# Sixteen unrolled turns rewritten as a hardware loop with staggered semaphore resets, in a log-softmax backward kernel

## The chip, the cores and the metric

The kernel runs on one core of one Trainium2 chip. The metric is the device time of one execution in microseconds (us), the median of several. Before the change it is 1867 us. Profiles are of one execution.

## The reference

The inputs are `y` (a log-softmax) and `dy`, both 8 x 1024 x 8192 float32. The output has the same shape.

```python
def reference(y, dy):
    softmax_x = np.exp(y)
    sum_dy = np.sum(dy, axis=-1, keepdims=True)
    return (dy - softmax_x * sum_dy).astype(np.float32)
```

Each input is 268 MB and has to be read once; the output is as large and has to be written once. That makes 805 MB, and one exponential, one multiply and two adds per element, one of them for the sum.

## The kernel before

The 8192 rows are cut into 32 groups of 256 rows: 128 partitions with two rows (R = 2) each, so one tile of a group is 128 x 16384 float32, 8.39 MB. There are two tiles for `dy` (`x_ts`), for even groups ("A") and odd groups ("B"), which also hold the result, and one buffer for `y`. A group's sum of `dy` is taken by VectorE for the first row of a partition and by ScalarE for the second. Then, piece by piece, ScalarE takes the exponential of `y` in place and VectorE writes exp(y) * (-sum) + dy over `dy`. Two groups share the `y` buffer, so the two halves of B's `y` are loaded as soon as the pieces of A's `y` that lie there have been used. All transfers are issued from SyncE.

```python
    def load_dy(g, x):
        nc.sync.dma_start(out=x[:], in_=dy_v[g])

    def load_y(g, at, lo, hi):
        nc.sync.dma_start(out=y_t[:, at + lo : at + hi], in_=y_v[g][:, lo:hi])

    def compute(x, s_t, at, r, pieces):
        for b, e in pieces:
            xs = slice(r * D + b, r * D + e)
            ys = slice(at + r * D + b, at + r * D + e)
            nc.scalar.activation(y_t[:, ys], y_t[:, ys], EXP)
            nc.vector.scalar_tensor_tensor(
                out=x[:, xs], in0=y_t[:, ys], scalar=s_t[:, r : r + 1],
                in1=x[:, xs], op0=ALU.mult, op1=ALU.add)

    for g in range(0, G, 2):                  # 16 turns, unrolled
        load_dy(g, x_ts[0])
        load_y(g, SHIFT, 0, W)
        s_t = sums(x_ts[0])
        for r in range(R):
            compute(x_ts[0], s_t, SHIFT, r, PIECES_A)
        load_dy(g + 1, x_ts[1])
        s_t = sums(x_ts[1])
        for r in range(R):
            load_y(g + 1, 0, r * D, (r + 1) * D)
            compute(x_ts[1], s_t, 0, r, PIECES_B)
        for j in range(2):
            nc.sync.dma_start(out=out_v[g + j], in_=x_ts[j][:])
    # ... (cut: views, pools, sums())
```

Of the kernel before, what the change touches and what calls it, by code (L numbers as in the profile page):

```python
# [1 line left out]

# [5 lines left out]


EXP = mybir.ActivationFunctionType.Exp  # L10
COPY = mybir.ActivationFunctionType.Copy
ALU = mybir.AluOpType


@with_exitstack
def kernel(
    ctx: ExitStack,
    tc: tile.TileContext,
    y: bass.AP,
    dy: bass.AP,  # L20
    out: bass.AP,
):





    nc = tc.nc
    P = nc.NUM_PARTITIONS
    fp32 = mybir.dt.float32  # L30

    N, D = y.flatten_outer_dims().shape
    R = 2
    W = R * D
    G = N // (P * R)
    assert N == G * P * R and D == 8192 and G % 2 == 0
    SHIFT = 3840

    PIECES_A = [(0, 1024), (1024, D - SHIFT), (D - SHIFT, D)]
    PIECES_B = [(0, 2048), (2048, 5120), (5120, D)]  # L40

    y_v = y.flatten_outer_dims().rearrange("(g p r) d -> g p (r d)", p=P, r=R)
    dy_v = dy.flatten_outer_dims().rearrange("(g p r) d -> g p (r d)", p=P, r=R)
    out_v = out.flatten_outer_dims().rearrange("(g p r) d -> g p (r d)", p=P, r=R)

    pool = ctx.enter_context(tc.tile_pool(name="pool", bufs=1))
    stats = ctx.enter_context(tc.tile_pool(name="stats", bufs=3))
    x_ts = [pool.tile([P, W], fp32, name=f"x{j}") for j in range(2)]
    y_t = pool.tile([P, SHIFT + W], fp32, name="y_t")

    def load_dy(g, x):
        nc.sync.dma_start(out=x[:], in_=dy_v[g])  # L52

    def sums(x):
        s_t = stats.tile([P, R], fp32, name="s_t")
        second_t = stats.tile([P, 1], fp32, name="second_t")
        nc.vector.tensor_reduce(  # L57
            out=s_t[:, 0:1], in_=x[:, :D], axis=mybir.AxisListType.X, op=ALU.add, negate=True
        )
        nc.scalar.activation(x[:, D:], x[:, D:], COPY, accum_out=second_t[:])  # L60
        nc.vector.tensor_scalar(  # L61
            out=s_t[:, 1:2], in0=second_t[:], scalar1=-1.0, scalar2=None, op0=ALU.mult
        )
        return s_t
# [10 lines that stand above are left out]
                out=x[:, xs],  # L75
                in0=y_t[:, ys],
                scalar=s_t[:, r : r + 1],
                in1=x[:, xs],
                op0=ALU.mult,
                op1=ALU.add,  # L80
            )

    for g in range(0, G, 2):
        load_dy(g, x_ts[0])
        load_y(g, SHIFT, 0, W)
        s_t = sums(x_ts[0])
        for r in range(R):
            compute(x_ts[0], s_t, SHIFT, r, PIECES_A)
        load_dy(g + 1, x_ts[1])
        s_t = sums(x_ts[1])  # L90
        for r in range(R):
            load_y(g + 1, 0, r * D, (r + 1) * D)
            compute(x_ts[1], s_t, 0, r, PIECES_B)
        for j in range(2):
            nc.sync.dma_start(out=out_v[g + j], in_=x_ts[j][:])


# [1 line left out]
_INS = ['y', 'dy']  # L99
_OUTS = [((8, 1024, 8192), 'float32')]  # L100


# [23 lines left out]
```

## Time and profile before

| | before |
|---|---|
| time, median of 3 | 1867.12 us (1866.89 to 1867.31) |
| bytes over the transfer queue | 805.31 MB |
| queue's share of the span | 99.8% |
| VectorE busy, ScalarE busy | 46%, 37% |
| one turn of two groups | 116.4 us |

The kernel is bound by its transfers. In lines of the profile, DVE is VectorE, ACT is ScalarE, SPq is SyncE's instruction stream, which issues all transfers, L73 is line 73 of the kernel, and x6 means that six instructions stand in one line. A transfer has landed when its last part has arrived.

### The profile page before, as it was taken

The page shows a single profiled execution, that of the slowest core. Times are in us where ns is not written, and L with a number is a line of the kernel's source. Part 1 is how long each engine was busy: PE and PEld are TensorE (multiplying, and loading weights), DVE is VectorE, ACT ScalarE, POOL GpSimd, SP SyncE. Part 2 cuts the span into 40 slices and gives each one's busy share as a digit, 9 for nine tenths or more (in the row PEclk, how much of TensorE's full clock was granted, in tenths as well). Part 3 has the DMA queues.
Part 4 walks back from the last instruction along what each step waited for, and adds up shares of the span by engine and source line. Part 5 has one row for each costly group of instructions (what it writes and reads, how often), then busy time and mean ns, then how long its engine had stood idle before and what let it go on. Part 6 is the DMA issues. An engine that isn't in the chain of part 4 may idle for free.

```text
span 1866.1 us, 843 instructions
## 1 busy us (share of the span) xinstructions
DVE 857.9 (46%) x256; ACT 689.3 (37%) x257; POOL 0.2 (0%) x4
## 2 busy tenths in 40 slices
DVE  2907429074290742807328073280732806338163
ACT  2606326063260532605326053260523605235152
POOL 0000000000000000000000000000000000000000
DMA  9999999999999999999999999999999999999998
GB/s 427 427 427 427 431 444 429 427 434 443 427 434 438 425 435 442 428 429 431 440 431 430 438 427 436 437 440 427 430 438 435 428 437 428 438 435 434 434 428 386
DMA packets 16134, 805.36 MB, mean 432 GB/s; under 512 B 1792, under 2 KB 1792, under 8 KB 1792
## 3 DMA queue, kind: packets, MB, share of 16 engines
q1 hardware_dynamic: 16128, 805.31, 99.8%
q14 instruction: 6, 0.05, 0.0%
HBM read 536.87 MB, written 268.44 MB: 432 GB/s over the span
## 4 chain that ended last, share of the span: by engine, by line
DMA 65%; DVE 14%; another core or an unknown queue 10%; ACT 9%; issue 0%; DVEq 0%; ACTq 0%; SPq 0%
DMA x<-in_dy_dram 31%; DMA out_dram<-x 30%; DVE x L74 14%; ACT x L60 6%; ACT y_t L73 3%; DMA y_t<-in_y_dram 3%; DVEq L121 0%; ACTq L121 0%; SPq L52 0%; ACTq L73 0%; ACTq L60 0%
## 5 line engine op out<-in xcount | busy, mean ns | idle before, releaser
L74 DVE SCALAR_TENSOR_TENSOR x<-y_t,s_t,x 128x1024 f32<-128x1024 f32 (+2 forms) x192 | 579.4, 3059 | 257.5 <-ACT y_t L73 257.5
L57 DVE TENSOR_REDUCE s_t<-x 128x1 f32<-128x8192 f32 x32 | 277.8, 8682 | 721.9 <-DMA x<-in_dy_dram 721.9
L73 ACT ACTIVATE y_t<-y_t 128x1024 f32<-128x1024 f32 (+2 forms) x192 | 460.1, 2466 | 280.0 <-DMA y_t<-in_y_dram 280.0
L60 ACT ACTIVATE x<-x 128x8192 f32<-128x8192 f32 x32 | 225.0, 7030 | 863.2 <-DMA x<-in_dy_dram 863.2
L60 ACT ACTIVATION_READ_ACCUMULATOR x<-x 128x1 f32 x32 | 6.0, 187 | 0.0
L61 DVE TENSOR_SCALAR s_t<-second_t 128x1 f32<-128x1 f32 x32 | 4.6, 143 | 0.0
L60 ACT ACT_TABLE_LOAD x1 | 1.3, 1283 | 0.7 <-PEq L110 0.7
L110 POOL MEMSET const-uint8-127<- 128x1 uint8 x1 | 0.1, 102 | 0.0
L110 POOL MEMSET const-bfloat16-1.0<- 128x1 bf16 x1 | 0.1, 101 | 0.0
L110 POOL MEMSET const-float32-0.0<- 128x1 f32 x1 | 0.1, 98 | 0.2 <-issue 0.2
L110 POOL MEMSET const-float32-1.0<- 128x1 f32 x1 | 0.1, 98 | 0.0
## 6 DMA issues: line engine op xcount, KB each, us to landing
y_t<-in_y_dram SPq DMA_DIRECT2D x32, 4096.0 KB, 22.1
x<-in_dy_dram SPq DMA_DIRECT2D x32, 48.4
out_dram<-x SPq DMA_DIRECT2D x32, 32.6
y_t<-in_y_dram SPq DMA_DIRECT2D x16, 57.5
```

The source lines that it names most:

```text
L57: nc.vector.tensor_reduce(out=s_t[:, 0:1], in_=x[:, :D], axis=mybir.AxisListType.X, op=ALU.add, negate=True)
L60: nc.scalar.activation(x[:, D:], x[:, D:], COPY, accum_out=second_t[:])
L61: nc.vector.tensor_scalar(out=s_t[:, 1:2], in0=second_t[:], scalar1=-1.0, scalar2=None, op0=ALU.mult)
L73: nc.scalar.activation(y_t[:, ys], y_t[:, ys], EXP)
L74: nc.vector.scalar_tensor_tensor(out=x[:, xs], in0=y_t[:, ys], scalar=s_t[:, r : r + 1], in1=x[:, xs], op0=ALU.mult, op1=ALU.add,)
L110: nc = _bacc.Bacc("TRN2", target_bir_lowering=False, num_devices=1)
```

## The change

The intent is a short program: one body in a hardware loop in place of sixteen copies. The loop that is built resets its semaphores, the counters by which engines wait for each other, between turns. Instead of a full barrier at the loop's end, the staggered form cuts the body into four stages with `stage_boundary()`. In the built program an engine enters a stage only when all engines have signalled the end of the stage two back, and a stage's semaphores are reset meanwhile.

```diff
-    for g in range(0, G, 2):
+    with tc.For_i(0, G, 2, iteration_sync="staggered") as g:
         load_dy(g, x_ts[0])
         load_y(g, SHIFT, 0, W)
+        tc.stage_boundary()
         s_t = sums(x_ts[0])
         for r in range(R):
             compute(x_ts[0], s_t, SHIFT, r, PIECES_A)
         load_dy(g + 1, x_ts[1])
+        tc.stage_boundary()
         s_t = sums(x_ts[1])
         for r in range(R):
             load_y(g + 1, 0, r * D, (r + 1) * D)
             compute(x_ts[1], s_t, 0, r, PIECES_B)
+        tc.stage_boundary()
         for j in range(2):
             nc.sync.dma_start(out=out_v[g + j], in_=x_ts[j][:])
```

What it builds to around the stores, told from the built program (waits and signals; "stage 1" is compute A and the load of B's dy, counted from 0):

```
SyncE    wait B's dy landed; signal "I have finished stage 1"
SyncE    wait until all five engines have signalled stage 1
SyncE    store A
SyncE    wait store A landed
SyncE    store B (waits for VectorE's last step of compute B)

VectorE  ... last step of compute B (stage 2)
VectorE  signal "I have finished stage 1"
ScalarE  ... last exponential of compute B (stage 2)
ScalarE  signal "I have finished stage 1"
```

## The prediction

> **What bounds the kernel now.** I read the page first. Its engine line, the DMA line of the forty slices, the queue line and the memory line are:
>
> ```profile
> DVE 857.9 (46%) x256; ACT 689.3 (37%) x257; POOL 0.2 (0%) x4
> DMA  9999999999999999999999999999999999999998
> q1 hardware_dynamic: 16128, 805.31, 99.8%
> HBM read 536.87 MB, written 268.44 MB: 432 GB/s over the span
> ```
>
> No engine is busy for half of the span, while the one transfer queue has work for 99.8% of it. The time is the bytes: 805.31 MB in 1866.1 us. What matters about any change here is whether the queue ever runs empty.
>
> Second, the timeline of one turn of two groups from the middle (start, duration, engine). A start behind "<-DMA" marks a landing.
>
> ```profile
> 857.53 14.32 ACT L73 ACTIVATE y_t<-y_t 128x1024 f32<-128x1024 f32 x6 [12.23 <-DMA y_t<-in_y_dram]
> ...
> 865.20 9.25 SPq L67 DMA_DIRECT2D y_t<-in_y_dram  x2
> 876.83 7.03 ACT L60 ACTIVATE x<-x 128x8192 f32<-128x8192 f32 x1 [4.98 <-DMA x<-in_dy_dram]
> ...
> 878.25 30.03 SPq L95 DMA_DIRECT2D out_dram<-x  x2
> ...
> 886.54 7.22 ACT L73 ACTIVATE y_t<-y_t 128x2048 f32<-128x2048 f32 x3 [2.59 <-DMA y_t<-in_y_dram]
> ...
> 896.56 7.22 ACT L73 ACTIVATE y_t<-y_t 128x2048 f32<-128x2048 f32 x3 [2.80 <-DMA y_t<-in_y_dram]
> ...
> 915.87 0.34 SPq L52 DMA_DIRECT2D x<-in_dy_dram  x1
> ...
> 935.16 0.33 SPq L52 DMA_DIRECT2D x<-in_dy_dram  x1
> ...
> 954.50 8.69 DVE L57 TENSOR_REDUCE s_t<-x 128x1 f32<-128x8192 f32 x1 [46.60 <-DMA x<-in_dy_dram]
> ...
> 973.91 14.32 ACT L73 ACTIVATE y_t<-y_t 128x1024 f32<-128x1024 f32 x6 [12.22 <-DMA y_t<-in_y_dram]
> ```
>
> The landings are: y of group A at 857.5, dy of group B 876.8, the two halves of y of B 886.5 and 896.5, store A 915.9, store B 935.2, the next dy of A 954.5, its y 973.9. An 8.39 MB transfer takes 19.3 to 19.4 us behind another, and a turn takes 116.4 us. The issues (SPq) show how far ahead the queue is fed. The halves of y of B are issued at 865.2 and about 874.1, the first 11.6 us before the transfer ahead of it lands. Store A is issued at 878.25, 18.3 us before the last half lands; store B at 908.28 minus the issue's 0.34, so 7.9 us before store A lands; the next dy of A at 915.87, 19.3 us before store B lands. The queue always holds a next transfer.
>
> Third, the start of the kernel, where the queue is empty:
>
> ```profile
> 0.73 0.38 SPq L52 DMA_DIRECT2D x<-in_dy_dram  x1
> ...
> 22.47 8.69 DVE L57 TENSOR_REDUCE s_t<-x 128x1 f32<-128x8192 f32 x1 [22.47 <-DMA x<-in_dy_dram]
> ...
> 41.80 14.32 ACT L73 ACTIVATE y_t<-y_t 128x1024 f32<-128x1024 f32 x6 [12.21 <-DMA y_t<-in_y_dram]
> ```
>
> From issue to landing the first load takes 21.74 us; the one behind it lands 19.33 us later. So a transfer issued into an empty queue costs 2.4 us more than one that is queued. Fourth, the waits of the transfer queue:
>
> ```profile
> SPq L95 <- DVE x L74: 526.6, 32, 30.0
> SPq L52 <- DMA out_dram<-x: 386.4, 30, 18.5
> ```
>
> Stores wait for VectorE's result, and loads of dy wait for the store that frees their tile. No store waits for another store.
>
> [...] a semaphore instruction that stands behind a 3840-element VectorE operation ran at 864.79, and that operation started at 865.09; the exponential it waited for had ended at 864.75. [...]
>
> **The change, part by part.** I read the built program's order, with waits and signals.
>
> *Removed:* fifteen copies of the body. Instruction fetches go over another queue and amount to 0.05 MB: nothing to gain.
>
> *Added, small:* a branch per turn, address arithmetic on SyncE before each transfer, a table load on ScalarE in each turn (1.28 us in the trace), handled while ScalarE waits some 51 us for dy. The branch on SyncE comes after store B is issued, with 19.3 us of it still to run. All hidden. [...]
>
> *Moved waits:* the body has four stages: loads of A; compute A and load dy of B; load y of B and compute B; both stores. An engine enters a stage only when every engine has signalled the end of the stage two back. ScalarE and VectorE give that signal at their next boundary in program order, after the last instruction of the stage. I go through the issues, with times counted from the landing of y of A (857.5).
>
> 1. First half of y of B. In before it needs three VectorE steps (7.7 us). Now it also needs ScalarE and VectorE to have dispatched all of compute A; the last exponential ends at 14.3. VectorE's signal then runs at once, by the early semaphore instruction above. With 0.3 us for SyncE's own semaphore steps, issue at 14.6. dy of B lands at 19.3, so 4.7 us are left: over the 2.4 us. The second half needs a VectorE step that ends at 16.5, as before. No loss, and the lead is thin.
>
> 2. Store A. In before it needs compute A, at 20.7. Now SyncE may enter the stores' stage only when ScalarE and VectorE have signalled the end of compute A, and that signal stands behind compute B in their order. Compute B's last exponential ends 7.2 us after the last half of y of B lands (896.56 plus 7.22 in the timeline). By then the queue has been empty since that landing. The store is issued at 7.3 + 0.3 = 7.6 us after that landing, and lands 21.7 later: 29.3, where before it landed 19.3 after it. Loss: 10.0 us per turn.
>
> 3. Store B. The built program has a new wait in front of it: the semaphore of store A. My reading is that addresses computed from the loop's register are not known to be disjoint. Store B therefore starts on an empty queue after store A has landed: 2.4 us per turn.
>
> 4. The next dy and y of A are issued right behind store B; dy of B waits for store B's landing, as before, with 38.7 us queued. No loss.
>
> Sum: 10.0 + 2.4 = 12.4 us per turn, in all sixteen turns, since every turn has its stores: 198 us. [...] 2067 us, a turn of about 128.8 us.
>
> **Rivals.** *The stagger is free,* as intended: 1868 to 1875 us. For it: branch, resets and table load have tens of us of slack, and three of the four stage gates ask for nothing late. Against it: the stores' gate comes due after the queue's last entry has landed. It holds only if that signal is given earlier than its place in the program.
>
> *Only one of the two losses counts.* If store A's delay alone costs: 1867 + 160 = 2028. If the store-behind-store wait alone: 1867 + 39 = 1907.
>
> *The first half of y of B comes late too.* If VectorE signals only when its last operation of compute A has ended (20.7), issue is at 21.0 and the queue is empty from 19.3: 4.1 us more per turn; the same delay at compute B (its last operation ends 50.3, 4 us after the exponential) adds another 4: 2067 + 130 = 2197. The early semaphore instruction in the trace speaks against it.
>
> *Instruction fetch at the branch.* [...] no run yet shows a branch, and it has 19.3 us to hide in.
>
> **Range and chances.** The sum rests on durations in the trace; the uncertain terms are the SyncE steps [...], whether VectorE signals before its last operation starts (0.7 us later if not), and whether a store into an empty queue costs 2.4 us as a load does[...]. A turn may lose 11.5 to 13.9 us: 2051 to 2090. Range 2048 to 2092. Faster by over 2%[...]: 0.01. Within 2%: 0.05, if the gate or signal is not where I read it. Slower: 0.94.
>
> **What would show it.** Right: turns of about 128.8 us; store A issued some 7.6 us after the last half of y of B landed, with the SyncE wait put to VectorE or ScalarE there; two holes in the queue in each turn, of about 9 and 2 us; store B issued within 0.1 us of store A's landing; DMA share near 90%; DVE and ACT busy unchanged but for the table loads. Wrong: stores issued before the last half lands (first rival), or a hole before the first half of y of B.

What no trace or run of this case shows is cut out of the prediction, and the cuts are marked. From the sum two terms are gone: 1 us for the loop's entry and a little for SyncE's extra steps, both guesses. The terms that stand make 1867 + 198 = 2065 us; with the two it came to the 2067 us that stand there. The turn's 11.5 to 13.9 us and the range are the author's estimate. The 0.3 us for SyncE's steps was a guess as well; in the trace of after they take 0.34 us in front of store A (984.57 to 984.91). That a branch stalls on an instruction fetch was not shown.

## More of the kernel before

The quickest way to see whether a stage feeds the queue is the table by stretches of the span: borders and length in us, busy time of VectorE, ScalarE and GpSimd (number of instructions), TensorE's clock, the share of the transfer engines that were busy, and GB/s. These two stretches of a middle turn of the kernel before are the landing of B's dy to that of the last half of B's y, and the 7.8 us after it, in which ScalarE still works on that half:

```profile
876.80:896.50 19.70, 17.79 (x6) 14.34 (x5) 0.00 (x0) 1.00 1.04 446
896.50:904.30 7.80, 6.88 (x3) 7.22 (x3) 0.00 (x0) 1.00 1.05 454
```

While the engines work on the last half, the queue moves 454 GB/s: store A, which was issued long before, is on its way. (A packet counts whole in the stretch in which it starts. That is why a share can come out above 1, and rates of such short stretches are rough.)

## The result

| | before | after |
|---|---|---|
| median (lowest to highest), 4 runs each | 1867.21 us (1866.89 to 1867.93) | 2052.17 us (2052.06 to 2052.82) |
| ratio | | 1.0991, 95% interval 1.0972 to 1.1010 |

Ratios are the mean time of one kernel's runs over that of the other's of the same rounds, so not quite the ratio of the medians quoted. Losses "per turn" below are the difference of the medians, divided by 16: here (2052.17 - 1867.21) / 16 = 11.56 us.

The page of the kernel after, the lines that answer to the four shown first of before:

```profile
DVE 857.9 (42%) x256; ACT 708.5 (35%) x272; POOL 0.2 (0%) x4
DMA  9899798998989989899898997989979899798997
q1 hardware_dynamic: 16128, 805.31, 91.5%
HBM read 536.87 MB, written 268.44 MB: 393 GB/s over the span
```

VectorE does the same work to the tenth of a microsecond. ScalarE has 15 instructions and 19.2 us more, the table loads. The bytes are the same. What has changed is the queue, which is busy for 91.5% of the span.

The timeline of a middle turn after the change (start, duration, engine):

```profile
938.42 14.32 ACT L73 ACTIVATE y_t<-y_t 128x1024 f32<-128x1024 f32 x6 [12.22 <-DMA y_t<-in_y_dram]
...
953.18 2.17 SPq L67 DMA_DIRECT2D y_t<-in_y_dram  x2
957.77 7.03 ACT L60 ACTIVATE x<-x 128x8192 f32<-128x8192 f32 x1 [5.03 <-DMA x<-in_dy_dram]
...
977.26 7.22 ACT L73 ACTIVATE y_t<-y_t 128x2048 f32<-128x2048 f32 x3 [2.56 <-DMA y_t<-in_y_dram]
...
984.91 21.23 SPq L98 DMA_DIRECT2D out_dram<-x  x2
1006.90 0.35 SPq L52 DMA_DIRECT2D x<-in_dy_dram  x1
...
1028.04 1.28 ACT L60 ACT_TABLE_LOAD   x1 [43.56 <-ACTq L83]
1028.29 0.33 SPq L52 DMA_DIRECT2D x<-in_dy_dram  x1
1046.94 7.03 ACT L60 ACTIVATE x<-x 128x8192 f32<-128x8192 f32 x1 [17.61 <-DMA x<-in_dy_dram]
```

The last half of B's y lands at 977.26. In before, store A was issued 18.3 us ahead of that landing; here it is issued at 984.91, 7.65 us behind it, just when the exponentials (7.22 us) are over. The line of the two stores lasts 21.23 us: store B is issued at 1005.79, as soon as store A has landed. The table load and the branch stand where nothing waits for them: the next dy of A is issued 0.76 us after the issue of store B is over (1006.14 to 1006.90), with store B still to run.

The stretches show what that does to the queue:

```profile
957.80:977.20 19.40, 17.44 (x6) 14.31 (x5) 0.00 (x0) 1.00 0.94 405
977.20:985.00 7.80, 7.12 (x3) 7.22 (x3) 0.00 (x0) 1.00 0.00 0
985.00:1005.70 20.70, 3.61 (x2) 0.00 (x0) 0.00 (x0) 1.00 0.94 405
1005.70:1028.00 22.30, 0.00 (x0) 0.00 (x0) 0.00 (x0) 1.00 1.02 423
```

In the 7.8 us in which before moved 454 GB/s, nothing moves. In the trace's packets the hole is 9.1 us in each turn, and there is a second one of 1.33 us between the two stores.

The waits of the transfer queue, for the stores and for the stage gates (line 83 is the loop):

```profile
SPq L98 <- DMA out_dram<-x: 324.7, 16, 20.3
SPq L83 <- DMA out_dram<-x: 285.1, 15, 19.3
SPq L83 <- DMA x<-in_dy_dram: 38.5, 16, 2.4
```

The first is the new wait of store B for store A, sixteen times. The gate in front of store A, the costliest wait of all, is in no line of this view. It waits for a count to fall below one, and the profile finds no releaser for that. It is to be seen in the chain that ended last, as time in which "issue" waits for nothing:

```profile
957.79 26.79 issue
...
984.91 20.74 DMA out_dram<-x
```

From the landing of B's dy (957.79) to the issue of store A, 27 us.

Whose signal the gate waited for is in the trace's semaphore events, which none of these views prints. ScalarE's runs 0.17 us after the last half of B's y has landed, while its exponentials still run. VectorE's runs 7.35 us after that landing, in each of the sixteen turns: at 984.53, just after the last exponential has ended (984.48) and before VectorE's last step starts (985.20). So it is VectorE's signal that holds the gate. It stands behind a step that waits for the last exponential.

The trace also records when each transfer's last part lands. The mean time from the landing before it, over turns 2 to 16 of the profiled run, in us:

| kernel | dy A | y A | dy B | y B, 1st half | y B, 2nd half | store A | store B | turn |
|---|---|---|---|---|---|---|---|---|
| before | 19.35 | 19.35 | 19.41 | 9.71 | 9.79 | 19.40 | 19.32 | 116.33 |
| after | 19.35 | 19.35 | 19.35 | 9.71 | 9.71 | 28.49 | 21.84 | 127.81 |

The turn is 11.48 us longer: 9.09 at store A and 2.52 at store B, less 0.13 elsewhere.

### The profile page after: what moved, and what is told of

It is laid out like the page before. It is cut to its first block, busy times and chain, and to the rows that moved or that the text cites. A ratio compares the mean times of both kernels' runs of the same rounds, so it can differ in the third digit from the quotient of the medians.

```text
span 2050.3 us, 2048 instructions
## 1 busy us (share of the span) xinstructions
DVE 857.9 (42%) x256; ACT 708.5 (35%) x272; POOL 0.2 (0%) x4
## 3 DMA queue, kind: packets, MB, share of 16 engines
q1 hardware_dynamic: 16128, 805.31, 91.5%
## 4 chain that ended last, share of the span: by engine, by line
DMA 48%; issue 21%; another core or an unknown queue 11%; DVE 10%; ACT 8%; SPq 1%; DVEq 0%; ACTq 0%
DMA x<-in_dy_dram 29%; DMA out_dram<-x 15%; DVE x L74 10%; ACT x L60 5%; DMA y_t<-in_y_dram 3%; ACT y_t L73 2%; SPq L98 0%; SPq L67 0%; SPq L83 0%; SPq L52 0%; SPq L124 0%; DVEq L83 0%; ACTq L73 0%
```

## The experiments

All eleven runs gave results that agree with the reference. "Before" was run on the same chip (1867.5 to 1868.2 us).

### The two waits without the loop

If the two waits are the cause, they must cost the same in the unrolled kernel. Small copies of 64 bytes were put on SyncE to wait for the same things, and the order of its transfers was kept as written.

```diff
+    with tc.manual_schedule(engines={mybir.EngineType.SP}):
         for g in range(0, G, 2):
             # ... as before
+            nc.sync.dma_start(out=late_t[:], in_=y_t[0:1, W - 16 : W])    # u1, u3
             nc.sync.dma_start(out=out_v[g], in_=x_ts[0][:])
+            nc.sync.dma_start(out=seen_t[:], in_=out_v[g][0:1, 0:16])     # u2, u3
             nc.sync.dma_start(out=out_v[g + 1], in_=x_ts[1][:])
```

The first (u1) makes only store A late.

> The unrolled kernel of before, no loop; transfers kept in program order on SyncE, and a 64-byte copy that waits for compute B's last exponential put in front of store A, so that store A is issued as late as in the loop. Theory: the first hole appears without any loop, loss per turn 7.2 (exponentials) + 0.4 (the small copy's issue) + 1.4 to 2.4 (restart) = 9.0 to 10.0 us: 2011 to 2027 us. Rival (the loop's own steps cause the loss): 1867 to 1873 us.

Measured: 2034.72 us (2034.33 to 2035.04), ratio 1.0894 (1.0876 to 1.0913): 10.45 us per turn, 8 us in all above the upper end expected. The 0.4 us expected for the small copy's issue is an estimate, near the issues of dy in before (0.33 to 0.42 us); here it stands in front of store A for 0.6 us, and store B, which waits for no landing here, lands 20.23 us behind store A where before has 19.32 (means of turns 2 to 16). The timeline of this run:

```profile
842.32 7.22 ACT L74 ACTIVATE y_t<-y_t 128x2048 f32<-128x2048 f32 x3 [2.55 <-DMA y_t<-in_y_dram]
...
849.56 0.51 SPq L96 DMA_DIRECT2D late_t<-y_t  x1
850.17 0.53 SPq L97 DMA_DIRECT2D out_dram<-x  x1
853.69 0.34 SPq L98 DMA_DIRECT2D out_dram<-x  x1
871.15 0.34 SPq L53 DMA_DIRECT2D x<-in_dy_dram  x1
```

Store A is issued 7.85 us after the last half lands, as late as in the loop, and store B 3.5 us behind it, without a wait. No loop is needed for the hole.

The second (u2) makes only store B wait for store A.

> The unrolled kernel of before with a 64-byte read of store A's rows between the two stores, which must wait for store A to land; nothing else. Theory: only the second hole appears: 1.4 to 2.4 us per turn plus up to 0.4 for the small copy's issue: 1890 to 1912 us.

Measured: 1924.94 us (1924.46 to 1925.56), ratio 1.0308 (1.0291 to 1.0325): 3.59 us per turn. That is a miss: 13 us above the upper end. The effect is there without the other and without a loop, but larger than I had it. Its landings (means of turns 2 to 16) put 2.77 us at store B (22.09 against 19.32), and 0.84 at the second half of B's y (10.63 against 9.79), where I had expected nothing.

The third (u3) has both.

> Both of these in the unrolled kernel. Theory: the two waits alone make the time of the loop: 11.5 us per turn and up to 0.8 for the two small copies' issues against some 0.5 us of SyncE steps that the loop has: 2045 to 2062 us. Rival (part of the loss is the loop's own): clearly below 2040 us.

Measured: 2061.87 us (2061.70 to 2062.20), ratio 1.1041 (1.1023 to 1.1059), on the upper end of what the theory said. (The 0.5 us of SyncE's steps in it are to be seen in the trace of after: 0.34 in front of store A, 984.57 to 984.91, and 0.13 in front of store B, 1005.66 to 1005.79.) Two waits without any loop cost 12.15 us per turn, the loop 11.56; the small copies, each with an issue on SyncE in front of a store, would account for the difference of 0.6: it stands at the two stores (28.87 and 22.06 us in the landings, against 28.49 and 21.84 in the loop). The other five landings are within 0.1 us of before's, so the kept order of transfers by itself costs nothing. The rival, that part of the loss is the loop's own, would have needed less than 2040.

### Taking the waits out of the loop

First, store A is moved before the last boundary, so that no gate stands in front of it.

```diff
             compute(x_ts[1], s_t, 0, r, PIECES_B)
+        nc.sync.dma_start(out=out_v[g], in_=x_ts[0][:])
         tc.stage_boundary()
-        for j in range(2):
-            nc.sync.dma_start(out=out_v[g + j], in_=x_ts[j][:])
+        nc.sync.dma_start(out=out_v[g + 1], in_=x_ts[1][:])
```

> Only the store of group A moves, from behind the last stage boundary to before it, so that no stage gate stands in front of it. Theory (late stage signal): the 9.1 us hole between the last half of y and store A closes, store A is issued when compute A ends, before that half lands; only store B's wait for store A's landing is left, 1.4 to 2.4 us per turn (the difference between the whole loss of 11.5 and 9.1 to 10.1 for the first hole): 1890 to 1906 us. Rival (the loop itself costs: branch, register-computed addresses, semaphore resets on SyncE): the store's place doesn't matter, 2040 to 2052 us.

Measured: 1918.59 us (1918.39 to 1919.06), ratio 1.0270 (1.0253 to 1.0287): 3.15 us per turn. Its timeline:

```profile
901.23 0.35 SPq L96 DMA_DIRECT2D out_dram<-x  x1
...
920.16 7.22 ACT L73 ACTIVATE y_t<-y_t 128x2048 f32<-128x2048 f32 x3 [3.37 <-DMA y_t<-in_y_dram]
...
939.58 0.35 SPq L98 DMA_DIRECT2D out_dram<-x  x1
```

Store A is issued 18.9 us before the last half lands, so the first hole is gone, and with it 134 us. The rival's 2040 is out. What is left is again more than the 1.4 to 2.4 us that I gave the second hole, and the time is 13 us above the upper end expected: a miss, as u2 was.

Second, the places stay, but store B's dependency on store A is declared absent. They write different rows.

```diff
-        for j in range(2):
-            nc.sync.dma_start(out=out_v[g + j], in_=x_ts[j][:])
+        st = [nc.sync.dma_start(out=out_v[g + j], in_=x_ts[j][:]) for j in range(2)]
+        tc.declare_no_dep(st[1].ins, st[0].ins, reason="rows of group g and of group g + 1")
```

> The kernel after, with the dependency of store B on store A declared absent (they write different rows). Stage boundaries as they were. Theory: the second hole of 1.3 us closes, the first of 9.1 stays; loss per turn 9.1 to 10.1 us: 2013 to 2029 us. If the store-behind-store wait cost nothing: 2052 us.

Measured: 2027.86 us (2027.73 to 2028.39), ratio 1.0856 (1.0838 to 1.0874): 9.98 us per turn, within what was expected. The wait's removal saves 1.58 us per turn. In its timeline the two stores are issued within 4.07 us, still behind the exponentials of the last half:

```profile
966.66 7.22 ACT L73 ACTIVATE y_t<-y_t 128x2048 f32<-128x2048 f32 x3 [2.56 <-DMA y_t<-in_y_dram]
...
974.31 4.07 SPq L97 DMA_DIRECT2D out_dram<-x  x2
```

Third, both edits at once.

> Both edits together: store A before the last boundary and no dependency between the stores. Theory: both holes close, the queue never runs empty, and branch, address arithmetic, table load and resets are hidden: 1866 to 1871 us. Rival (the loop itself costs something per turn): above 1880 us.

Measured: 1873.53 us (1869.72 to 1880.62), ratio 1.0035 (1.0008 to 1.0061). Of 185 us, 180 are gone, so branch, address arithmetic, resets and table load are hidden. But the median lies between the two theories' ranges, and the scatter is 11 us where before's is 1. That rest is taken up below.

The two losses don't add: 9.98 and 3.15 make 13.1, and together they cost 11.56. The landings say where the difference is:

| kernel | 1st half | 2nd half | store A | store B | turn |
|---|---|---|---|---|---|
| before | 9.71 | 9.79 | 19.40 | 19.32 | 116.33 |
| after | 9.71 | 9.71 | 28.49 | 21.84 | 127.81 |
| store A earlier (s1) | 9.72 | 10.52 | 19.35 | 21.82 | 119.50 |
| no store wait (s2) | 9.71 | 9.71 | 28.53 | 20.28 | 126.29 |

Store B takes 2.5 us more than in before in both kernels that have the wait, close to what was predicted. But only about 1.5 of it goes with the wait: in s2, where the wait is gone, store B still takes 20.28, 1.0 more than in before. The last turn tells what the 1.0 goes with, for there no load is queued behind store B. In the kernel after it lands 20.74 us after its issue in that turn, and 21.74 to 22.05 in the fifteen others. In s2 it takes 19.34 in that turn, and 20.3 to 20.4 in the others. In before, with loads behind it too, it takes 19.63 in the first turn and about 19.3 in most later ones.

In s1 another 0.8 us stands at the second half. In the kernel after, nothing is queued behind that half, and it takes 9.71. In s1 store A is queued behind it, and it takes 10.52. In before, store A is queued behind that half too, but it takes 10.62 us only in the first turn, 10.17 in the second, and 9.7 in most later ones. So the turn from loads to stores costs about 0.8 us, and that from stores to loads about 1.0, in kernels that empty the queue in every turn, and in before mostly at the start. The 1.0 is counted twice in 13.1, and the 0.8 is in s1 alone: that is the difference, within 0.2 us. One thing that goes with it is how close the sixteen transfer engines are: they land their parts of a transfer within 0.4 us in the first turn of before and 3.7 us apart in its last ones (4.5 at the last two stores), while an empty queue brings them back to 0.7 us or less by the landing of store B in every turn of s1. But that alone doesn't explain it: in the second turn of the run with both edits they are 0.5 us apart, and the second half takes 9.71 us. The cause of the 0.8 and of the 1.0 us stays open.

### The place of the signal

In the fourth run stores and boundaries stay where the kernel after has them. Only ScalarE's and VectorE's signals that compute A is finished are placed by hand, behind B's sums in place of the end of compute B.

```diff
         s_t = sums(x_ts[1])
+        tc.previous_stage_wait(mybir.EngineType.Activation)
+        tc.previous_stage_wait(mybir.EngineType.DVE)
         for r in range(R):
             load_y(g + 1, 0, r * D, (r + 1) * D)
```

> Stores and boundaries as in the kernel after; only ScalarE's and VectorE's signals that compute A is finished are placed just behind the sums of group B instead of at the end of compute B. Theory (the place of the signal in program order is the cause): store A is issued some 7.5 us after dy of B lands, about 12 us before the last half of y lands, the first hole closes, store B's wait stays: the same as the run with store A moved, 1890 to 1906 us. Rival (it is the boundary in front of the stores, or SyncE's own steps there, not the signal): 2040 to 2052 us.

Measured: 1918.86 us (1918.61 to 1919.69), ratio 1.0271 (1.0254 to 1.0289), the same as with store A moved, and over the stated range for the same reason. The timeline:

```profile
899.87 7.03 ACT L60 ACTIVATE x<-x 128x8192 f32<-128x8192 f32 x1 [5.03 <-DMA x<-in_dy_dram]
...
907.43 32.53 SPq L100 DMA_DIRECT2D out_dram<-x  x2
```

Store A is issued 7.56 us after B's dy lands, as foretold, although it stands behind the boundary. The boundary costs nothing (1918.86 us behind it, 1918.59 with store A in front of it); the place of the signal does. Both engines' signals were moved; whether VectorE's alone would have done was not run.

With that, and the dependency declared absent as well, the loop should lose nothing whatever its stages:

> Stores and boundaries where the kernel after has them; signals of compute A early, and no dependency between the stores. Theory: the place of the signal and the store dependency are the whole loss, whatever the stages are: as the kernel with both edits, 1869 to 1880 us.

Measured: 1871.91 us (1871.79 to 1875.22), ratio 1.0027 (1.0013 to 1.0042). It is as expected.

### The plain loop

The same loop without stages, with the default barrier at its end (`tc.For_i(0, G, 2)`, the three boundaries removed).

> The same hardware loop with the default full barrier at its end in place of staggered resets, without stages. Theory: without stage gates store A is issued when compute A ends, so no first hole; store B still waits for store A's landing (1.4 to 2.4 us); and the barrier empties the queue once a turn behind store B: about 2.4 us for the restart[...]. Loss 5 to 9 us per turn: 1947 to 2011 us, faster than the staggered loop. If staggering hid anything here, it would be slower than 2052 us.

Measured: 1961.65 us (1960.69 to 1961.87), ratio 1.0504 (1.0487 to 1.0522), as expected. (A guess for the barrier is cut from the expectation's sum: without it, 1.4 to 2.4 and 2.4 make 3.8 to 4.8 of the 5 to 9 us per turn.) The barrier that staggering was to avoid is 90 us faster than staggering with these boundaries. Its timeline around the loop's end:

```profile
958.63 0.35 SPq L95 DMA_DIRECT2D out_dram<-x  x1
980.48 1.28 ACT L60 ACT_TABLE_LOAD   x1 [34.04 <-PEq L83]
980.65 0.35 SPq L52 DMA_DIRECT2D x<-in_dy_dram  x1
...
1002.45 7.03 ACT L60 ACTIVATE x<-x 128x8192 f32<-128x8192 f32 x1 [20.69 <-DMA x<-in_dy_dram]
```

Store B, into an empty queue and with nothing behind it, lands 20.76 us after its issue; the next load is issued 1.26 us after that and takes 21.8 us. The queue's hole at the loop's end is 2.6 us in the packets. It is paid once a turn, besides store B's wait for store A, whose hole of 1.33 us is here too. The gate in front of store A held the queue empty for 9.1.

### The last five microseconds

The kernel with both edits still lost about 5 us and scattered. Its first half of B's y is issued only 4.6 us before B's dy lands, which is the thin lead of the prediction's first step. In before that lead is 11.6 us. The lead that counts may be that of the fastest transfer engine: it shrinks from 4.1 us in the first turn to 1.9 in the eighth, as the engines drift apart. The next kernel adds to both edits an early signal for the first stage, too:

```diff
         s_t = sums(x_ts[0])
+        tc.previous_stage_wait(mybir.EngineType.Activation)
+        tc.previous_stage_wait(mybir.EngineType.DVE)
         for r in range(R):
             compute(x_ts[0], s_t, SHIFT, r, PIECES_A)
```

> The kernel with both edits (store A before the last boundary, no dependency between the stores), and in addition the signals that the first stage is finished placed right behind the sums of group A, so that the first half of y of B is issued 7.7 us after y of A lands, as in the unrolled kernel, and not 14.5 us after it. Theory (the 5 us that the kernel with both edits still lost come from that thin lead: from the eighth turn on the fastest transfer engine is 2 to 3 us ahead, the lead before it is 1.9 to 2.8 us, and the halves of y take 9.83 and 9.93 us on the mean where before had 9.71 and 9.79): 1867 to 1870 us, no more than 2 us above before, halves of y back at 9.7 and 9.8. Rival (the loop's own steps on SyncE cost the rest): 1872 to 1876 us.

> The kernel with both edits once more, on the same chip as the run with the first gate moved, since its four times scattered from 1869.7 to 1880.6 us: 1870 to 1878 us, again with a wider scatter than before's.

Measured: 1868.82 us (1868.49 to 1869.74), ratio 1.0007 (0.9994 to 1.0019), against 1873.50 us (1871.10 to 1879.93), ratio 1.0036 (1.0024 to 1.0048), for the repeat with both edits alone. Both are as expected. The queue's share cannot show the difference: it is 99.8% here as in before, and 99.9% in the repeat.

The two halves of B's y together take 19.50 us in before, 19.44 in this kernel, and 19.76, 19.81 and 19.80 in the three profiled runs with the thin lead (both edits, the repeat, and the run with early signals and no store wait, s5). So the late issue is worth the last five microseconds, and the scatter goes with it. That the fastest engine runs dry is the likely way, but no run shows it: in the repeat it is the second half that is longer (10.10), not the first (9.71).

No run is faster than before, and there is little left to win: six transfers of 19.35 us make 116.1 us, and a turn takes 116.3.

## Why the prediction was right

- *The bound.* Right. Busy time of VectorE is unchanged. Of the 11.5 us per turn, 9.1 and 1.33 are holes in the queue, and about 1.0 is a later landing of store B with a load behind it.
- *Hidden parts.* Right. Branch, addresses and table load cost nothing that the best loop kernel shows: 1868.82 against 1867.95 us. The compare-and-branch on SyncE takes 49 ns at the median in the trace of after, and the next issue follows 0.76 us after store B's. The loop's entry delays the first load from 0.73 to 1.97 us, by 1.2 us once.
- *Step 1, first half of y of B.* Issued 14.76 us after y of A lands (14.6 predicted), and landed 9.71 us after B's dy: no loss in the kernel after. In before this issue needs two VectorE steps (the second ends at 865.17), not the three that the prediction names; its 7.7 us are right. "The lead is thin" became true only where the queue never empties: there it costs about 5 us in all.
- *Step 2, store A.* Issue 7.65 us after the last half's landing (7.6 predicted). The early signal of VectorE was right too: it runs at 984.53, and VectorE's last operation ends at 988.61. The restart was mis-sized: I took 2.4 us from the first load of the kernel, and store A lands 20.74 us after its issue in an empty queue, which is 1.4 us over 19.35. So the loss is 9.1 us, not 10.0. That first load has other transfers queued behind it and store A has none; store B takes 21.77 us from its issue with a load queued behind it, and 20.74 in the last turn without one. Whether this is the reason for the first load's 21.74, no run shows.
- *Step 3, store B.* The wait was right: store B is issued 0.1 us after store A's landing, and the wait is store B's dependency on store A: declared absent, it is gone. The size, 2.5 us lost against 2.4 predicted, agrees in part by luck: the restart is 1.5, and 1.0 stays when the wait is gone (s2).
- *Sum.* 12.4 us per turn predicted, 11.5 measured, nearly all of the difference in store A's restart. 2067 us predicted, 2052 measured, near the lower end of the range.
- *What would show it.* Holes of 9 and 2 us: 9.1 and 1.33. Turn of 128.8: 127.8. Share of the queue near 90%: 91.5%. Wrong in one point: I expected the view of waits to put SyncE's wait down to VectorE or ScalarE. It shows no such line; the wait is "issue" in the chain.
- *Rivals.* A free stagger is refuted by the result, but describes the loop once its signals are placed well and the stores' dependency is declared absent. That only one loss counts is refuted too: each stays when the other is taken away (s1, s2). Its 2028 us for store A's delay alone is what s2 measured, by luck: from 9.1 and 1.0 us per turn, not from 10.0. Both of its sums are 1 us above their terms (1867 + 160 is 2027, 1867 + 39 is 1906). The first half of y of B does not come late: VectorE's signals run before its last operations, as step 1 had it. Of a stall at the branch, the rival of instruction fetch, the trace shows nothing: SyncE's branches take 64 ns at most.

## What to carry to other kernels

In a loop whose resets are staggered, look for where each engine signals that it has left a stage, not only at where the boundaries stand: an engine whose signal stands behind a step of the next stage that still waits for a transfer signals late, and the queue's issuer pays (here VectorE's runs 7.35 us after the landing, and the queue is empty for 9.1 us per turn). Check in the built program that no transfer which was issued ahead of time now stands behind such a gate, and that addresses computed from the loop's register have not made two independent stores dependent (here 1.58 us per turn). Where the bound is a transfer queue, judge a control-flow change by the lead of each issue over the landing ahead of it.
